# A hybrid decoder layer on one core: attention outputs copied by VectorE, a norm's scaling put last in its step, keys written a step later

## The chip, the core and the metric

The kernel runs on one core of a Trainium2 chip. The core has five engines that run at the same time, each through its own list of instructions in order: TensorE (PE, with its weight loads shown as PEld) multiplies matrices into PSUM banks; VectorE (DVE) and ScalarE (ACT) work on whole tiles of 128 partitions and can read PSUM; GpSimd (POOL) does element-wise work in SBUF; SyncE (SP) starts the DMA transfers. Engines wait for each other through semaphores. The metric is the device time of one execution in microseconds (us). Three runs of the kernel before gave 1030.6, 1030.78 and 1031.11; their median, 1030.78 us, is the time to compare with.

## The reference

One layer of a decoder on a sequence of 512 positions and a width of 1024, all in float32:

```python
u = rmsnorm(x, ln1_g)
q, k, v, pool_in, z, xbc, dt_raw, gate_pre = split(u @ w_in)
y_a = dilated_attention_mixer(q, k, v, rel_bias) @ w_a   # three groups of 6 heads, dilation 1, 4, 16
y_b = pool_mixer(pool_in, pool_w, pool_scale) @ w_b      # causal means over 2, 4, 8, 16 positions
y_c = ssd_mixer(z, xbc, dt_raw, ...) @ w_c               # state space scan in chunks of 128
gates = sigmoid(gate_pre + b_gate)
x = x + (gates[0] * y_a + gates[1] * y_b + gates[2] * y_c) @ w_o
x = x + conv_ffn(rmsnorm(x, ln2_g), ...)
return rmsnorm(x, final_g)
```

In the attention, each group's output `o` and the log-sum of its scores are computed by themselves, and the three outputs are summed with softmax weights over the groups. In the state space branch the result `y` is multiplied by `silu(z)`, normed over each of two halves of 512 channels (`y * rsqrt(mean(y*y) + eps) * norm_w`), and then multiplied by `w_c`.

## The kernel before

Every large product is done in three matmuls: each operand is split into a high half (a cast to a shorter float format, `wh`, `uh`, `ah`, `yth`) and a low half (the difference, `wl`, `ul`, `al`, `ytl`), and high x high, high x low and low x high are summed in PSUM (`mm3`, whose matmuls have line 237). Weights come as *jobs*: a DMA fetches a job's weights (`fetch`, L184), ScalarE casts the high half (`cast`, L196), VectorE subtracts to get the low half (`lows`, L216), and the job's body issues the matmuls. While one job's matmuls are issued, the next job's low half, the cast of the one after and the fetch of the one after that are issued ahead of them (`prepare`).

Smaller work is cut into generators. A job's body calls `step()` after each chunk of matmuls. A step takes one new generator from the list `waiting` into the list `running`, and moves each running generator on by one stretch, in the order of that list. Within the step there are phases: what stands before any other yield runs first, then what follows `yield ROWS`, then `yield WHOLE`, and last `yield REST`. A bare `yield` ends the generator's part of this step. `after(n, it)` lets n steps go by before `it` begins. Casts that were put off (`second`) are issued at the start of a step. Four engines run exactly in the order in which these Python lines issue instructions, so moving a line changes what each engine does first.

Tiles of 128 x 512 come from one pool of 54 slots, PSUM banks from two tags of four (`mm` for the chunks, `sm` for the small work). A new tile takes a slot that has come free and waits for its last reader.

Three places matter here:

- **Keys of the second attention group** (`qk_sevens(1)`). Queries and keys of dilation 4 are computed with seven half-size products in place of eight. The jobs run in the order A11, 4, A12, 1, 2, 3, A22. Job 2's evacuation is `p6`: VectorE adds the product to `r1` (L702), then `emit("k", 0, ...)` writes the first half of the keys, three additions of 128 x 256 in all (L695). Job 3's evacuation `p7` does the same for the second half (L707, L695), and A22 writes the second half of the queries. Gate jobs and the scores of `attend(1)` follow.
- **Outputs of the attention** (`attend(g)`). A pair of heads gives its scores (L743), which get their bias (L758), maximum (L762) and exponential (L765), are transposed (L772, copied out at L773) and multiplied by the values into a bank `po` (L784). L790 copies that bank to `o`, for groups 1 and 2 with the positions put back in their order. The third group (g = 2) runs between gate jobs and the items of the state space scan (`ssd_item`): transposes `pxs` (L1025), products `py` (L1070) and `pyo` (L1077), and on VectorE L1040, L1047, L1079, L1080, L1083.
- **Norm of the state space branch** (`y_norm(gi)`, once for each half). ScalarE casts the sum of squares, VectorE makes its low half (L1127), two matmuls with ones sum it over the partitions, ScalarE does Ln, Exp and Square (L1135 to L1137), VectorE refines (L1140, L1141). Two steps later the loop at L1144 scales two of four tiles of `y` (L1146), ScalarE casts them (L1148), and the next step subtracts for the low halves (L1153) before it scales the other two. Around the same time `combine` weights the attention outputs on GpSimd (L835), `split_o(c)` adds the three groups (L841, VectorE), casts `ah` (L843, ScalarE) and subtracts `al` (L846, VectorE), for the product with `w_a`. The product with `w_c` comes after that.

Of the kernel before, what the change touches and what calls it, by code (L numbers as in the profile page):

```python
# [83 lines left out]
def trunk(ctx: ExitStack, tc, out, x, rel_bias, ln1_g, w_in, b_gate, w_a, pool_w, pool_scale, w_b,  # L84
# [492 lines left out]
    def blocked(ap, g):  # L577
        return ap.rearrange("p (r j) -> p r j", r=4) if g == 0 else perm(ap, g)
# [71 lines left out]
    def qk_sevens(g):  # L650


        W = []
        quarter = lambda two, h: w_in[:, (C_Q, C_K)[h] + 384 * g:(C_Q, C_K)[h] + 384 * g + 384].rearrange(
            "(k two p) c -> two p k c", two=2, p=P)[two]
        chunks = ((0, 1), (2,))
        r1, r2, r3, r5 = {}, {}, {}, {}

        def load():
            for two in range(2):  # L660
                W.append(ypool.tile([P, 4, S], F32, name="w3", tag="xs")[:, :, :384])
                sp.dma_start(W[two], quarter(two, 1))

        def job(j, raw, form, use):
            def body(ws):
                wh, wl = ws
                parts = side_u(j)
                for i, ms in enumerate(chunks):
                    ps = MM("pq")
                    for n, m in enumerate(ms):  # L670
                        o = slice(m * P, (m + 1) * P)
                        mm3(ps[:, 256 * n:256 * n + 256], lambda k: wh[:, k, o], lambda k: wl[:, k, o],
                            lambda k: parts[k][0], lambda k: parts[k][1], range(4))
                    use(i, ps[:, :256 * len(ms)])
                step()
            new = Job([raw] if raw is not None else [], 4, 384, body)
            new.form = form
            if raw is None:
                new.load = lambda: None
            return new  # L680

        def keep(r):
            def use(i, ps):
                r[i] = T("rq")[:, :ps.shape[-1]]
                act.copy(r[i], ps)
            return use

        def emit(which, hi, i, a, b):

            for n, m in enumerate(chunks[i]):  # L690
                if (which, g, m) not in QK:
                    QK[which, g, m] = T(f"{which}{g}")
                view = (grouped if which == "q" else plain)(QK[which, g, m], g)
                piece = lambda t: perm(t[:, 256 * n:256 * n + 256], g)
                dve.tensor_tensor(view[:, :, 64 * hi:64 * hi + 64], piece(a), piece(b), OP.add)  # L695

        def p5(i, ps):
            keep(r5)(i, ps)
            dve.tensor_tensor(r2[i], r2[i], ps, OP.add)

        def p6(i, ps):
            dve.tensor_tensor(r1[i], r1[i], ps, OP.add)  # L702
            emit("k", 0, i, r1[i], r2[i])

        def p7(i, ps):
            r3[i] = T("rq")[:, :ps.shape[-1]]
            dve.tensor_tensor(r3[i], r1[i], ps, OP.add)  # L707
            emit("k", 1, i, r3[i], r5[i])

        one = job("A11", quarter(0, 0), None, keep(r1))  # L710
        two = job("A12", quarter(1, 0), None, lambda i, ps: emit("q", 0, i, r1[i], ps))
        three = job(4, None, lambda: W[1], keep(r2))
        one.then = lambda: diff(one.raw, W[0], one.raw)
        three.then = lambda: diff(W[0], W[1], W[0])
        two.then = lambda: diff(W[1], W[1], one.raw)
        return load, [one, three, two, job(1, None, lambda: one.raw, p5), job(2, None, lambda: W[1], p6),
                      job(3, None, lambda: W[0], p7), job("A22", None, lambda: diff(two.raw, two.raw, W[1]),
                                                          lambda i, ps: emit("q", 1, i, r3[i], ps))]

    def attend(g):  # L720
        nm, ls = both[:, :, :HEADS], both[:, :, 32:]
        if g == 0:
            banks = [[(1, 0, 2), (2, 1, 2)], [(3, 2, 2), (0, 0, 1)]]
        else:
            banks = [[(n, n, 1) for n in range(4)]]
        outs, probs, scores = {}, {}, {}

        def item(h, nb, bank):
            c, hh = h // 2, h % 2
            b = bias_of(g, h)  # L730
            off, spans = 0, []
            for n, kb, w in bank:
                spans.append((n, kb, w, off))
                off += w * P
            if hh == 0:

                q, k = QK["q", g, c], QK["k", g, c]
                yield ROWS
                pss = [SM("ps"), SM("ps")]
                for n, kb, w, o in spans:  # L740
                    for i in range(2):
                        r = slice(DH * i, DH * i + DH)
                        pe.matmul(pss[i][:, o:o + w * P], q[r, n * P:(n + 1) * P],  # L743
                                  k[r, kb * P:(kb + w) * P], start=True, stop=True)
                scores[c, nb] = pss
            yield REST
            ps = scores[c, nb][hh]
            total = off
            sb = T("sb")
            if g == 0 and total == 384:  # L750
                dve.tensor_tensor(sb[:, :256], ps[:, :256], b, OP.add)
                dve.tensor_tensor(sb[:, 256:384], ps[:, 256:384], b[:, P:], OP.add)
                for n, kb, w, off in spans:
                    dve.tensor_reduce(nm[:, n, h:h + 1], sb[:, off:off + w * P],
                                      AX.X, OP.max, negate=True)
            else:
                n = len(bank)
                dve.scalar_tensor_tensor(sb.rearrange("p (n c) -> p n c", n=n),  # L758
                                         ps.rearrange("p (n c) -> p n c", n=n), 0.125 if g == 1 else 1.0,
                                         b.unsqueeze(1).to_broadcast([P, n, S // n]), OP.mult, OP.add)  # L760
                n0 = bank[0][0]
                dve.tensor_reduce(nm[:, n0:n0 + n, h], sb.rearrange("p (n c) -> p n c", n=n),  # L762
                                  AX.X, OP.max, negate=True)
            for n, kb, w, off in spans:
                act.activation(sb[:, off:off + w * P], sb[:, off:off + w * P], AF.Exp,  # L765
                               bias=nm[:, n, h:h + 1], accum_out=ls[:, n, h:h + 1])
            yield
            yield
            yield WHOLE
            pt = SM("pt")  # L770
            for o in range(0, total, P):
                pe.transpose(pt[:, o:o + P], sb[:, o:o + P], eye)  # L772
            (act.copy if h % 2 else dve.tensor_copy)(sb[:, :total], pt[:, :total])  # L773
            probs[h, nb] = sb
            if h % 2 == 0:
                return
            yield
            if c not in outs:
                outs[c] = SM("po")
            po = outs[c]  # L780
            for n, kb, w, off in spans:
                for i in range(w):
                    for hh in range(2):
                        pe.matmul(po[DH * hh:DH * hh + DH, n * P:(n + 1) * P],  # L784
                                  V[g, kb + i][:, (2 * c + hh) * DH:(2 * c + hh + 1) * DH],
                                  probs[2 * c + hh, nb][:, off + i * P:off + (i + 1) * P],
                                  start=i == 0, stop=i == w - 1)
            if nb == len(banks) - 1:
                o = T(f"o{g}")
                act.copy(blocked(o, g), grouped(po, g))  # L790
                OT[g, c] = o

        def stats():
            yield WHOLE
            ps = SM("pst")
            for n in range(4):
                pe.transpose(ps[:32 + HEADS, n * P:(n + 1) * P], both[:, n, :], eye)
            for at, store, nme in ((0, NM, "nmT"), (32, LS, "lsT")):
                t = store[g] = T(nme)
                dve.tensor_copy(blocked(t[:HEADS], g), grouped(ps[at:at + HEADS], g))  # L800

        fill([item(2 * c + hh, nb, bank) for c in range(3) for nb, bank in enumerate(banks)
              for hh in range(2)] + [after(2, stats())])

# [316 lines left out]
    def y_norm(gi):  # L1121
# [20 lines left out]
        yield  # L1142
        yield
        for j in range(4):  # L1144
            y, m = Y[gi][:, j, :], 4 * gi + j
            dve.scalar_tensor_tensor(y, y, cst["dgc"][:, 8 + m:9 + m], r, OP.mult, OP.mult)  # L1146
            yh, yl = T("yth", F32R), T("ytl", F32R)
# [566 lines left out]
```

## Time and profile before

| | |
|---|---|
| median of three runs | 1030.78 us |
| the profiled execution's own time | 1031.29 us |
| its span, first to last instruction | 1029.5 us |
| TensorE busy | 1018.4 us (99%) |
| VectorE busy | 709.0 us (69%) |
| ScalarE busy | 494.1 us (48%) |
| GpSimd busy | 129.2 us (13%) |
| mean granted TensorE clock | 0.998 |

In the rows of the timeline the first two numbers are the start from the beginning of the span and the time that the row covers, both in us. Then come engine, line, operation, what is written and read, shapes, and how many instructions the row merges; in brackets is the time for which the engine stood idle before it and what it waited for. Rows of merged instructions run from the start of the first to the end of the last. Matmuls overlap in the pipeline, so that a single one of 512 columns shows 0.39 us while the next starts 0.23 us after it. Rows of groups have a count, the busy time and mean, or for one line the least, the median and the greatest duration in ns.

### The profile page before, as it was taken

The numbers are of one execution on the slowest core, as the hardware profiler recorded it, in microseconds if no ns is written. First come the engines' busy times: TensorE is split into PE (matmuls) and PEld (weight loads), VectorE is DVE, ScalarE is ACT, GpSimd is POOL, SyncE is SP. The second block draws the span as 40 slices with busy tenths as digits, with TensorE's granted clock in tenths as the row PEclk, the third lists the DMA queues.
The fourth block names the chain that finished last, engine by engine and source line by source line (L and its number), as shares of the span: only waits on it lengthen the run. The fifth ranks groups of instructions, "written<-read, shape, count | busy, mean of one in ns | idle before, by whom it ended". The sixth has DMA issues, their size and how long they took to land.

```text
span 1029.5 us, 13279 instructions
## 1 busy us (share of the span) xinstructions
PE 1018.4 (99%) x5282; PEld 859.5 (83%) x5282; DVE 709.0 (69%) x940; ACT 494.1 (48%) x790; POOL 129.2 (13%) x108
## 2 busy tenths in 40 slices
PE   9999999999999999999999999999999999999997
PEld 8998877899888888878887888898888888888885
DVE  6553566788756659676788756767778668685756
ACT  6432545454674364567576333545444434433434
POOL 1770000000000001000043501101111100111002
PEclk9999999999999999999999999999999999999999
DMA  8444312124422354542253625543232233421322
GB/s 258 148 127 140 104 61 75 31 87 139 123 82 82 87 150 111 144 132 61 77 160 120 199 82 206 176 143 114 82 123 82 84 118 109 140 82 41 123 82 82
DMA packets 113356, 117.62 MB, mean 114 GB/s; under 512 B 5235, under 2 KB 97206, under 8 KB 113295
## 3 DMA queue, kind: packets, MB, share of 16 engines
q1 hardware_dynamic: 112703, 115.92, 36.7%
q8 instruction: 41, 0.67, 0.3%
q10 hardware_dynamic: 592, 0.86, 0.2%
q14 instruction: 20, 0.16, 0.1%
HBM read 112.97 MB, written 2.22 MB: 112 GB/s over the span
## 4 chain that ended last, share of the span: by engine, by line
PE 90%; DVE 5%; ACT 3%; DMA 1%; issue 1%; ACTq 0%; DVEq 0%
PE pa L237 29%; PE pu L237 22%; PE pb L237 12%; PE pd L237 7%; PE pqk L237 6%; PE pa L1565 2%; PE pq L237 2%; PE pu L1369 1%; PE ps L743 1%; PE pt L772 1%; PE ppw L237 1%; PE po L784 1%; DMA al<-ad 1%; DVE xs L1146 1%; DVE wl L216 1%
## 5 line engine op out<-in xcount | busy, mean ns | idle before, releaser
L216 DVE TENSOR_TENSOR wl<-raw,wh 128x2048 fp32r<-128x2048 f32 (+3 forms) x95 | 220.3, 2320 | 52.9 <-ACT wh L196 44.1
L196 ACT CAST wh<-raw 128x1024 fp32r<-128x1024 f32 (+3 forms) x188 | 187.7, 1018 | 47.6 <-DVE raw L341 18.0
L1264 DVE SCALAR_TENSOR_TENSOR hc<-pu,fcol,hc 128x510 f32<-128x510 f32 x88 | 65.8, 748 | 55.6 <-ACT hc L1261 54.0
L237 PE MATMUL pa<-uh,wh 128*128 128x512 f32 x384 | 97.5, 396 | 0.0
L237 PE MATMUL pa<-ul,wh 128*128 128x512 f32 x384 | 94.9, 389 | 0.0
L237 PE MATMUL pa<-uh,wl 128*128 128x512 f32 x384 | 94.8, 389 | 0.0
L237 PEld LDWEIGHTS pa<-ul,wh 128*128 128x128 f32 x384 | 72.1, 188 | 15.1
L237 PEld LDWEIGHTS pa<-uh,wl 128*128 128x128 f32 x384 | 72.1, 188 | 15.0
L237 PE MATMUL pu<-uh,wh 128*128 128x512 f32 (+1 forms) x352 | 83.6, 379 | 0.0
L237 PE MATMUL pu<-ul,wh 128*128 128x512 f32 (+1 forms) x352 | 83.5, 379 | 0.0
L237 PE MATMUL pu<-uh,wl 128*128 128x512 f32 (+1 forms) x352 | 83.5, 379 | 0.0
L237 PEld LDWEIGHTS pa<-uh,wh 128*128 128x128 f32 x384 | 70.3, 188 | 14.0
L237 PEld LDWEIGHTS pu<-ul,wh 128*128 128x128 f32 x352 | 64.2, 188 | 12.5
L237 PEld LDWEIGHTS pu<-uh,wl 128*128 128x128 f32 x352 | 64.2, 188 | 12.5
L237 PEld LDWEIGHTS pu<-uh,wh 128*128 128x128 f32 x352 | 64.1, 188 | 12.4
L1261 ACT ACTIVATE hc<-pu,fcol,fcol 128x512 f32<-128x512 f32 x40 | 31.2, 780 | 79.6 <-PE pu L237 79.6
L1269 POOL TENSOR_TENSOR hc<-hc 128x512 f32<-128x512 f32 x22 | 30.9, 1403 | 289.1 <-DVE hc L1264 226.1
L1053 POOL TENSOR_TENSOR st<-st,dts 128x512 f32<-128x512 f32 x4 | 6.8, 1707 | 381.2 <-ACT st L1061 320.7
L765 ACT ACTIVATE sb<-sb,nmls 128x128 f32<-128x128 f32 (+1 forms) x72 | 30.1, 419 | 31.1 <-DVE nmls L762 18.3
L1162 ACT ACTIVATE sg<-pa,col 128x512 f32<-128x512 f32 x24 | 16.5, 688 | 38.1 <-PE pa L237 34.0
L1266 ACT ACTIVATE hc<-hc 128x512 f32<-128x512 f32 x22 | 13.9, 632 | 40.1 <-DVE hc L1264 40.1
L907 DVE SCALAR_TENSOR_TENSOR xs<-pa,col,xs 128x509 f32<-128x509 f32 (+2 forms) x24 | 18.0, 749 | 18.7 <-ACT xs L903 18.2
(380 smaller groups left out, 1874.3 us busy)
## 6 DMA issues: line engine op xcount, KB each, us to landing
raw<-in_w_in_dram SPq DMA_DIRECT2D x25, 1024.0 KB, 5.8
raw<-in_ffn_w_up_dram SPq DMA_DIRECT2D x22, 1024.0 KB, 5.2
raw<-in_w_o_dram SPq DMA_DIRECT2D x8, 1024.0 KB, 6.3
raw<-in_ffn_w_down_dram SPq DMA_DIRECT2D x8, 1024.0 KB
raw<-in_w_in_dram SPq DMA_DIRECT2D x14, 512.0 KB, 4.0
raw<-in_w_in_dram SPq DMA_DIRECT2D x6, 768.0 KB
raw<-in_w_b_dram SPq DMA_DIRECT2D x4, 1024.0 KB, 5.1
al<-ad SPq DMA_DIRECT2D x16, 256.0 KB, 8.6
```

Source lines behind the costliest of these rows:

```text
L196: act.copy(job.high[:, :, o], job.raw[:, :, o])
L216: (eng or dve).tensor_tensor(l[:, :, o], job.raw[:, :, o], h[:, :, o].bitcast(F32), OP.subtract)
L237: pe.matmul(ps, l, r, start=first and n == 0, stop=last and n == total - 1, skip_group_check=onto)
L743: pe.matmul(pss[i][:, o:o + w * P], q[r, n * P:(n + 1) * P], k[r, kb * P:(kb + w) * P], start=True, stop=True)
L765: act.activation(sb[:, off:off + w * P], sb[:, off:off + w * P], AF.Exp, bias=nm[:, n, h:h + 1], accum_out=ls[:, n, h:h + 1])
L907: dve.scalar_tensor_tensor(t[:, sh:], ps[:, :S - sh], col[:, o_cw + 12 * k + m:o_cw + 12 * k + m + 1], t[:, sh:], OP.mult, OP.add)
L1162: act.activation(s, ps, AF.Sigmoid, bias=col[:, o:o + 1])
L1261: act.activation(t, ps, AF.Identity, bias=ff["c1"][:, ff["b"] + m:ff["b"] + m + 1], scale=fw(2, m))
L1264: dve.scalar_tensor_tensor(t[:, sh:], ps[:, :S - sh], fw(k, m), t[:, sh:], OP.mult, OP.add)
L1266: act.activation(t, t, AF.Silu)
L1269: pool.tensor_tensor(a, a, t, OP.mult)
L1565: pe.matmul(first[2 * n + j][:, lo:hi], a[:, k, j * P:(j + 1) * P], b[:, k, lo:hi], start=a is wh and b is uh and k == 0, stop=a is wl and ...
```

## The change

Three edits. The first half of the keys is no longer written in `p6`, but by a small generator that starts in the step after the one that ends job 2's body. The three copies of `o` of the third attention group go to VectorE in place of ScalarE. In `y_norm`, a `yield REST` stands ahead of the first and the third scaling, so that each pair of scalings with its casts is issued in the last phase of its step rather than at the generator's place in the first phase.

```diff
+        def later(i):
+            emit("k", 0, i, r1[i], r2[i])
+            return
+            yield
+
         def p6(i, ps):
             dve.tensor_tensor(r1[i], r1[i], ps, OP.add)
-            emit("k", 0, i, r1[i], r2[i])
+            running.append(after(1, later(i)))
...
             if nb == len(banks) - 1:
                 o = T(f"o{g}")
-                act.copy(blocked(o, g), grouped(po, g))
+                (dve.tensor_copy if g == 2 else act.copy)(blocked(o, g), grouped(po, g))
                 OT[g, c] = o
...
         for j in range(4):
+            if j % 2 == 0:
+                yield REST
             y, m = Y[gi][:, j, :], 4 * gi + j
             dve.scalar_tensor_tensor(y, y, cst["dgc"][:, 8 + m:9 + m], r, OP.mult, OP.mult)
             yh, yl = T("yth", F32R), T("ytl", F32R)
```

## The prediction

> **What bounds the kernel now.** The page comes first: one engine is busy nearly throughout.
>
> ```profile
> span 1029.5 us, 13279 instructions
> ...
> PE 1018.4 (99%) x5282; PEld 859.5 (83%) x5282; DVE 709.0 (69%) x940; ACT 494.1 (48%) x790; POOL 129.2 (13%) x108
> ```
>
> TensorE is idle for 1029.5 - 1018.4 = 11.1 us of the span. No edit here takes a matmul away, so time can only come out of places where TensorE stands still. The view of TensorE's waits lists these by releaser (columns: total us, times, longest us):
>
> ```profile
> PE uT L1582 <- DVE diag L1594: 1.3, 2, 0.9
> ...
> PE pxs L1025 <- ACT o L790: 0.9, 1, 0.9
> PE pa L237 <- DVE al L846: 0.6, 1, 0.6
> PE pq L237 <- DVE wl L216: 0.3, 1, 0.3
> ```
>
> The first row is the start of the kernel, which the change leaves alone. The other three are single stalls, one each: transposes waiting for ScalarE's copy of an attention output, the attention projection waiting for a low half `al`, and the last key/query product waiting for a low half of weights. Each edit touches the order of work in front of one of them. So the question is how much of each stall goes and whether something new takes its place. Since the end of a matmul in this trace is modelled, I measure stalls from start to start, which comes out larger than the idle time in that view.
>
> **Keys of the first half, a step later (p6, `later`).** Timeline at the stall:
>
> ```profile
> 258.22 3.47 ACT L196 CAST wh<-raw 128x768 fp32r<-128x768 f32 x4 [3.55 <-DVE raw L341]
> 258.76 1.19 DVE L695 TENSOR_TENSOR k<-rq 128x256 f32<-128x256 f32 x2
> 260.31 0.62 DVE L695 TENSOR_TENSOR k<-rq 128x256 f32<-128x256 f32 x1
> 260.85 1.75 DVE L216 TENSOR_TENSOR wl<-raw,wh 128x1536 fp32r<-128x1536 f32 x1
> 261.75 0.64 PE L237 MATMUL pq<-ul,wh 128*128 128x256 f32 x4
> 262.66 0.74 PE L237 MATMUL pq<-uh,wl 128*128 128x256 f32 x4 [0.27 <-DVE wl L216]
> 263.24 0.64 PE L237 MATMUL pq<-uh,wh 128*128 128x256 f32 x4
> 265.31 2.28 DVE L216 TENSOR_TENSOR wl<-raw,wh 128x2048 fp32r<-128x2048 f32 x1
> 269.77 1.97 PE L237 MATMUL pa<-uh,wl 128*128 128x512 f32 x8
> ```
>
> Groups of four such matmuls follow each other by 0.48 us where nothing waits: a group of four takes 0.64, of which the last matmul's tail overlaps the next group. From 261.75 two groups would bring the third to 262.71; it starts at 263.24. The stall with its restart costs 0.53 us. It ends when L216, the last job's split, ends at 262.60. In front of that split VectorE does three key writes, 1.19 + 0.62 = 1.81 us, and these are what moves. The split cannot go forward by all of it: it also needs ScalarE's cast. Of the four casts the first two are this job's, so by half of 3.47 us they are done near 259.95. The split then runs from about 259.95 to 261.70, before 262.23 when TensorE asks. The stall goes: gain 0.53.
>
> What comes later: the same three writes run at the end of the next step, between the other keys and the gate's split at 265.31. VectorE has gained nothing but a gap before the cast (260.85 - 259.95 = 0.9 earlier against 1.81 taken out), so that split ends 0.9 later, at 268.5 instead of 267.6. TensorE wants it at 269.77 - 0.53 = 269.24; 0.7 us of cover is left. The scores that read these keys come behind the gate's whole first chunk, whose last part starts at 269.77; the keys are written near 266.3 by then. No DMA is issued by the moved part, and no queue of SP or POOL is passed. Bounds of this term: 0.43 without the restart, 0.53 with it.
>
> **Outputs of the third group by VectorE (`attend(2)`, L790).** There are three such copies. The first is the one TensorE waits for; an undisturbed step is shown ahead of it.
>
> ```profile
> 442.00 1.16 PE L1077 MATMUL pyo<-xcv,st 128*128 128x128 f32 x8
> 442.99 0.60 PE L1025 MATMUL pxs<-eye,xs 128*128 128x128 f32 x4
> 443.35 0.94 PE L237 MATMUL pa<-uh,wh 128*128 128x512 f32 x3
> 457.06 1.04 PE L784 MATMUL po<-sb,vr 128*64 128x128 f32 x16
> 458.03 1.16 PE L1077 MATMUL pyo<-xcv,st 128*128 128x128 f32 x8
> 458.91 1.08 ACT L790 COPY o<-po 128x512 f32<-128x512 f32 x1
> 459.22 0.69 DVE L1079 TENSOR_TENSOR ea<-pyo,ea 128x512 f32<-128x512 f32 x1 [1.49 <-PE pyo L1077]
> 460.04 0.66 PE L1025 MATMUL pxs<-eye,xs 128*128 128x128 f32 x4 [0.86 <-ACT o L790]
> 460.45 0.71 PE L237 MATMUL pa<-uh,wh 128*128 128x512 f32 x2
> 464.55 0.68 DVE L1040 TENSOR_SCALAR al<-al,acs 128x128 f32<-128x128 f32 x3 [2.14 <-DMA al<-ad]
> ```
>
> From pyo to the next projection takes 443.35 - 442.00 = 1.35 us undisturbed and 460.45 - 458.03 = 2.42 here: 1.07 lost, because the transposes take over the bank of `po`, ScalarE, busy with other work, begins its copy only at 458.91. VectorE is idle just then (1.49). In the written order the copy stands ahead of L1047 and L1079, so VectorE goes to it when `po` ends at 457.06 + 1.04 = 458.10. How long does it take there? The same pattern (grouped in, blocked out) appears on VectorE for six rows, and plain copies out of PSUM on both engines:
>
> ```profile
> L800 DVE COPY lsT<-pst x3: 682/1049/1053, 194.6 to 504.9; 6x512 f32<-6x512 f32 x3
> L773 DVE COPY sb<-pt x12: 547/683/692, 132.6 to 492.9; 128x512 f32<-128x512 f32 x9, 128x384 f32<-128x384 f32 x3
> L773 ACT COPY sb<-pt x12: 451/577/590, 135.8 to 498.2; 128x512 f32<-128x512 f32 x9, 128x384 f32<-128x384 f32 x3
> ```
>
> I take 1.05 to 1.07, the nearest row: 458.13 to 459.20, transposes at 459.25 with the latency seen at 459.99 to 460.04. They start 0.79 earlier; 0.23 and the restart stay. Bounds: 683 ns would end before the transposes could start at all (gain 1.07). If VectorE is slower than ScalarE in the strided case as in the plain one, 683/577 x 1.08 = 1.28 us, the gain is 0.58. The Trainium skill speaks for this dearer price (VectorE: DVE Perf Modes, Specifications: ScalarE is placed closer to PSUM, VectorE closer to SBUF). The plain rows agree with it by 18%; with it the whole sum below would be 0.21 smaller, but the 1.049 row is strided and on VectorE, so I stay with that.
>
> What queues behind the waiting copy: L1047 (two multiplies), then L1079 and its followers, some 1.4 us later than now. L1040, which comes next, waits 2.14 for a DMA until 464.55 anyway, which covers it. ScalarE is rid of 1.08 three times, worth nothing alone: TensorE waits for none of the other two copies. They cost VectorE about 1.07 each, in steps for which the view of TensorE's waits has no row; should that cover be gone, each costs at most its 1.07.
>
> **Scaling last in its step (`y_norm`, `yield REST`).** The order of VectorE before the third stall:
>
> ```profile
> 544.29 3.48 DVE L1146 SCALAR_TENSOR_TENSOR xs<-xs,dgc,yr 128x512 f32<-128x512 f32 x2
> 547.70 3.48 DVE L841 TENSOR_TENSOR o<-o,o 128x512 f32<-128x512 f32 x2
> 553.30 1.28 DVE L1153 TENSOR_TENSOR ytl<-xs,yth 128x512 fp32r<-128x512 f32 x2
> 556.48 0.69 DVE L1140 SCALAR_TENSOR_TENSOR yt<-pss,yt 128x512 f32<-128x512 f32 x1 [1.89 <-ACT yt L1137]
> 564.25 1.41 DVE L1146 SCALAR_TENSOR_TENSOR xs<-xs,dgc,yr 128x512 f32<-128x512 f32 x2
> 564.46 0.84 PE L237 MATMUL pa<-ah,wh 128*128 128x512 f32 x3
> 565.14 0.61 PE L237 MATMUL pa<-al,wh 128*128 128x512 f32 x2
> 565.58 0.68 DVE L846 TENSOR_TENSOR al<-o,ah 128x512 fp32r<-128x512 f32 x1
> 566.32 0.50 PE L237 MATMUL pa<-al,wh 128*128 128x512 f32 x1 [0.56 <-DVE al L846]
> 566.65 0.63 PE L237 MATMUL pa<-ah,wl 128*128 128x512 f32 x2
> 581.66 1.98 PE L237 MATMUL pa<-yth,wh 128*128 128x512 f32 x8
> ```
>
> Three such matmuls take 565.14 - 564.46 = 0.68 start to start, so `ah,wl` was due at 565.82 and started at 566.65: 0.83 lost to the third `al` (565.58 to 566.26, wanted at 565.60). In that step two scalings, 1.41 us, run right ahead of it; last in the step they run behind it, and `al` is ready at 564.85. That alone suffices. The step at 544 helps too: `o` goes before the scalings, so ScalarE's `ah` and the Ln, Exp and Square behind it start some 3.4 us earlier and the 1.89 of waiting at L1140 goes. Against that, the two later low halves (L1153) now wait for casts that ScalarE does after these functions, by my count some 0.4 us at 553.3; net some 1.5 us earlier. So even with TensorE ahead by the other two gains (0.53 + 0.79 = 1.32, wanting `al` at 564.28) it is there at about 563.4. The scaled `y` is first read at 581.66, over ten microseconds after the last scaling, which is the cover for the delay. The moved scalings issue no DMA; their cast on ScalarE moves with them. Gain 0.83, bounds 0.56 to 0.83.
>
> **Sum.** 0.53 + 0.79 + 0.83 = 2.15 us. The profiled execution itself took 1031.29 (its span and 1.79 around it), so it would take 1029.14. The median of the runs is 0.51 below the profiled one: 1030.78 - 2.15 = 1028.63. Low ends 0.43 + 0.58 + 0.56 = 1.57 give 1029.2; high ends 0.53 + 1.07 + 0.83 = 2.43 give 1028.35.
>
> **Rivals.** (1) One stall stays because what it waits for is not earlier: most likely `al` (ScalarE's `ah` comes later than I counted) or the transposes (the copy starts late behind another VectorE operation). Against it: VectorE's idle 1.49 and the 1.41 that suffices by itself. One term of about 0.8 falls away: 1029.4. (2) The change doesn't do what it says: TensorE is early after each place, and asks early for the next split, cast or DMA, which hands all of it back; 1030.8. Against it: after the last stall no wait of TensorE is listed at all. (3) The other side: VectorE's tightest place, the gate's split with 0.7 us of cover. Tiles come from one pool of 54 slots in the order in which these come free, and the moved writes change who gets which; a write that lands on a slot whose last reader is late holds VectorE in front of that split. The longest wait that VectorE shows in front of a split is 7.7:
>
> ```profile
> DVE wl L216 <- ACT wh L196: 46.0, 32, 7.7
> ```
>
> Such a wait there would cost 7.7 - 0.7 = 7.0, and the sum 7.0 - 2.15 = 4.9 slower, 1035.6; it decides from 0.7 + 2.15 + 2.06 = 4.9 us of lateness. Nothing in the trace shows one.
>
> **How the numbers follow.** A measurement here tells about 0.2%, 2.06 us, from no change: the bound is 1028.72. All three stalls go: 0.72 (own range 1028.3 to 1029.2, as just worked out), and since its centre lies 0.09 below the bound with the dearer copy above it, 0.50 of that falls under the bound and 0.22 above. One stall stays: 0.15. All handed back: 0.05. Slower: 0.08. So faster 0.50, same 0.22 + 0.15 + 0.05 = 0.42, slower 0.08. The range 1028.1 to 1030.0 takes in the first two cases with 0.2 us for the scatter of the runs, and leaves out the last two and a little below.
>
> **What would show it.** In the changed kernel's waits of TensorE the rows for L237 <- L216 and L237 <- L846 are gone, and pxs waits 0.1 to 0.3 us for a VectorE copy of some 1.07 us that starts at the end of `po`. The three key writes stand after the second half's, and L216 for the last key/query job starts when its cast ends. I am wrong if TensorE's idle time falls by less than 1 us, if the copy takes over 1.3 us, or if a wait not in the list above appears behind 265 us.

## The result: 1.1 us, half of what was predicted

The changed kernel takes 1029.68 us (median of 22 runs, 1029.19 to 1030.25) beside 1030.80 us for the kernel before (22 runs, 1029.87 to 1031.76). The ratio is 0.9988, with an interval of 0.9983 to 0.9994: 1.12 us or 0.11% faster, which is less than the 0.2% that was set as the bound of no change. The interval is 0.6 to 1.8 us of gain; no gain at all lies outside it, and so do the 2.15 us of the prediction. The prediction was 1028.6, with a range of 1028.1 to 1030.0.

The two profiled executions say something else. The kernel before took 1031.29 and the changed one 1029.19, which is 2.10 apart and almost exactly the predicted 2.15. Why one pair of traces and the medians differ by a factor of two is what most of the experiments are about.

The page of the changed kernel (span, busy time, and its chain that ended last) shows the gain where it was looked for:

```profile
span 1027.4 us, 13279 instructions
...
PE 1017.5 (99%) x5282; PEld 859.4 (84%) x5282; DVE 710.5 (69%) x943; ACT 490.8 (48%) x787; POOL 129.1 (13%) x108
...
PE 98%; DMA 1%; DVE 0%; ACT 0%; ACTq 0%; issue 0%
```

The same line of the chain, on the page of the kernel before:

```profile
PE 90%; DVE 5%; ACT 3%; DMA 1%; issue 1%; ACTq 0%; DVEq 0%
```

TensorE's idle time fell from 11.1 us to 1027.4 - 1017.5 = 9.9. That is only 1.2 less, because part of each stall counts as busy: the busy time fell too, by 0.9, with the same 5282 matmuls. VectorE and ScalarE have left the chain. The view of TensorE's waits in the changed kernel has lost all three rows at issue and gained none; what is left is the start of the kernel:

```profile
PE uT L1589 <- DVE diag L1601: 1.7, 2, 1.1
PE pa L1530 <- DVE ones L1521: 1.1, 1, 1.1
```

Now the three places in the changed kernel's timeline, in the order of the prediction. Line numbers are 5 higher from L700 on and 7 higher from L1150 on. First the keys:

```profile
259.88 1.76 DVE L216 TENSOR_TENSOR wl<-raw,wh 128x1536 fp32r<-128x1536 f32 x1 [0.76 <-ACT wh L196]
261.81 0.64 PE L237 MATMUL pq<-ul,wh 128*128 128x256 f32 x4
...
262.77 0.64 PE L237 MATMUL pq<-uh,wh 128*128 128x256 f32 x4
263.81 2.24 DVE L695 TENSOR_TENSOR k<-rq 128x256 f32<-128x256 f32 x4
265.97 2.29 DVE L216 TENSOR_TENSOR wl<-raw,wh 128x2048 fp32r<-128x2048 f32 x1
269.31 1.07 PE L237 MATMUL pa<-uh,wl 128*128 128x512 f32 x4
```

Groups of four now follow by 0.48 us throughout (261.81, 262.29, 262.77). The group that started at 261.75 before starts at 261.81, and the one two later at 262.77 instead of 263.24: 0.47 + 0.06 = 0.53 gained. Then the copy:

```profile
456.59 1.04 PE L789 MATMUL po<-sb,vr 128*64 128x128 f32 x16
457.56 1.16 PE L1082 MATMUL pyo<-xcv,st 128*128 128x128 f32 x8
457.68 1.08 DVE L795 COPY o<-po 128x512 f32<-128x512 f32 x1 [4.37 <-PE po L789]
458.60 2.12 DVE L1052 TENSOR_TENSOR al<-al,cbt 128x512 f32<-128x512 f32 x2
458.81 0.66 PE L1030 MATMUL pxs<-eye,xs 128*128 128x128 f32 x4
459.23 2.08 PE L237 MATMUL pa<-uh,wh 128*128 128x512 f32 x8
```

VectorE starts the copy 0.05 us after `po` ends, and the transposes start 1.25 after `pyo` (458.81 - 457.56) where they started 2.01 after it (460.04 - 458.03). The next projection starts at 459.23 instead of 460.45: 1.22 earlier in all, 0.75 of it new here. And the norm:

```profile
541.87 3.48 DVE L846 TENSOR_TENSOR o<-o,o 128x512 f32<-128x512 f32 x2
545.27 3.48 DVE L1153 SCALAR_TENSOR_TENSOR xs<-xs,dgc,yr 128x512 f32<-128x512 f32 x2
553.18 0.68 DVE L1145 SCALAR_TENSOR_TENSOR yt<-pss,yt 128x512 f32<-128x512 f32 x1
560.95 0.68 DVE L851 TENSOR_TENSOR al<-o,ah 128x512 fp32r<-128x512 f32 x1
561.55 1.41 DVE L1153 SCALAR_TENSOR_TENSOR xs<-xs,dgc,yr 128x512 f32<-128x512 f32 x2
564.61 0.84 PE L237 MATMUL pa<-ah,wl 128*128 128x512 f32 x3
```

The sums `o` and their followers go ahead of the scalings, both at 541.87 and at 560.95. L1145 starts with no wait in front of it. The third `al` ends at 561.63. The group `ah,wl`, which stands right behind the matmul that reads it, starts at 564.61 instead of 566.65, 2.04 earlier, 0.82 of it new. So in these two executions the three terms are 0.53, 0.75 and 0.82, against 0.53, 0.79 and 0.83 predicted.

### The profile page after: what moved, and what is told of

The parts are those of the page before. It is cut to its first block, busy times and chain, and to the rows that moved or that the text cites. A ratio compares the mean times of both kernels' runs of the same rounds, so it can differ in the third digit from the quotient of the medians.

```text
span 1027.4 us, 13279 instructions
## 1 busy us (share of the span) xinstructions
PE 1017.5 (99%) x5282; PEld 859.4 (84%) x5282; DVE 710.5 (69%) x943; ACT 490.8 (48%) x787; POOL 129.1 (13%) x108
## 4 chain that ended last, share of the span: by engine, by line
PE 98%; DMA 1%; DVE 0%; ACT 0%; ACTq 0%; issue 0%
PE pa L237 36%; PE pu L237 22%; PE pb L237 12%; PE pd L237 7%; PE pqk L237 6%; PE pq L237 3%; PE pa L1572 2%; PE ps L748 1%; PE pu L1376 1%; PE pt L777 1%; PE po L789 1%; PE ppw L237 1%; PE py L1075 1%; DMA xin<-in_x_dram 1%; PE pyo L1082 1%; PE pst L1063 0%
## 5 line engine op out<-in xcount | busy, mean ns | idle before, releaser
L237 PE MATMUL pa<-uh,wh 128*128 128x512 f32 x384 | 97.5, 396 | 0.0
L237 PE MATMUL pa<-ul,wh 128*128 128x512 f32 x384 | 94.9, 389 | 0.0
L237 PE MATMUL pa<-uh,wl 128*128 128x512 f32 x384 | 94.8, 389 | 0.0
L237 PEld LDWEIGHTS pa<-ul,wh 128*128 128x128 f32 x384 | 72.1, 188 | 15.1
L237 PEld LDWEIGHTS pa<-uh,wl 128*128 128x128 f32 x384 | 72.1, 188 | 15.0
L237 PE MATMUL pu<-uh,wh 128*128 128x512 f32 (+1 forms) x352 | 83.6, 379 | 0.0
L237 PE MATMUL pu<-ul,wh 128*128 128x512 f32 (+1 forms) x352 | 83.5, 379 | 0.0
L237 PE MATMUL pu<-uh,wl 128*128 128x512 f32 (+1 forms) x352 | 83.5, 379 | 0.0
L237 PEld LDWEIGHTS pa<-uh,wh 128*128 128x128 f32 x384 | 70.3, 188 | 14.0
L237 PEld LDWEIGHTS pu<-ul,wh 128*128 128x128 f32 x352 | 64.2, 188 | 12.5
L237 PEld LDWEIGHTS pu<-uh,wl 128*128 128x128 f32 x352 | 64.2, 188 | 12.4
L237 PEld LDWEIGHTS pu<-uh,wh 128*128 128x128 f32 x352 | 64.1, 188 | 12.4
```

What stands on the lines that cost most here:

```text
L237: pe.matmul(ps, l, r, start=first and n == 0, stop=last and n == total - 1, skip_group_check=onto)
```

## The experiments

Two theories stood against each other in the end. By that of the prediction, each edit takes its own stall away, and the medians differ from the traces by scatter. By the other (D in the expectations, formed after the first four runs), the copies' stall is not a property of the kernel before but of its one traced execution. "Time" below is the median of 8 to 11 runs; the kernel before beside them gave medians of 1031.00, 1031.01 and 1031.06 (31 to 33 runs each). The lag from `pyo` to the transposes `pxs` is from start to start.

| kernel | time, us | ratio to before | pyo to pxs, us | split of keys late | third `al` late |
|---|---|---|---|---|---|
| before (traced once) | | 1 | 2.01 | yes | yes |
| the change, second trace | 1029.51 | 0.9985 (0.9977 to 0.9994) | 1.25 | no | no |
| keys alone | 1030.24 | 0.9993 (0.9984 to 1.0002) | 1.25 | no | yes |
| copies alone | 1030.34 | 0.9991 (0.9982 to 1.0000) | 1.25 | yes | no |
| norm alone | 1030.21 | 0.9992 (0.9983 to 1.0001) | 1.25 | yes | no |
| keys and norm | 1029.64 | 0.9989 (0.9980 to 0.9997) | 1.25 | no | no |
| 2 loads ahead, ScalarE copies | 1030.42 | 0.9994 (0.9985 to 1.0003) | 1.25 | yes | yes |
| 2 loads ahead, VectorE copies | 1030.02 | 0.9991 (0.9982 to 1.0000) | 1.25 | yes | no |
| 6 loads ahead, ScalarE copies | 1031.99 | 1.0007 (0.9998 to 1.0017) | 1.95 | yes | yes |
| 6 loads ahead, VectorE copies | 1030.21 | 0.9992 (0.9983 to 1.0002) | 1.27 | yes | no |
| norm, second half only | 1030.15 | 0.9989 (0.9979 to 1.0000) | 1.27 | yes | no |
| three products on GpSimd | 1030.02 | 0.9991 (0.9981 to 1.0002) | 1.25 | yes | no |
| the change, `uh` cast first | 1029.33 | 0.9985 (0.9976 to 0.9994) | 1.26 | no | no |

**Each edit alone, and the whole again.** The keys alone:

```diff
-            emit("k", 0, i, r1[i], r2[i])
+            running.append(after(1, later(i)))
```

> Only the keys' edit. Both theories expect the product that waited for the split (0.53 us late before) on time, and the gate's split behind it ending near 268.5 us, before TensorE asks. Theory S (the stalls are the same in every execution): the other two stalls stand in this trace as before, 1.07 us at the transposes and 0.83 us at the third al, and the time falls by 0.5 us. Rival V (the stalls vary from execution to execution, and the traced execution of before had long ones): one of those two differs from its value before by over 0.2 us, and the time falls by 0.3 us or less.

The copies alone:

```diff
-                act.copy(blocked(o, g), grouped(po, g))
+                (dve.tensor_copy if g == 2 else act.copy)(blocked(o, g), grouped(po, g))
```

> Only the copies' edit. Both theories: the first VectorE copy takes 1.05 to 1.1 us, starts when po ends, and the transposes are 0.2 to 0.35 us late instead of 1.07. S: the split stall (0.53) and the third al (0.83) stand as before; the time falls by 0.8 us. V: one of them differs by over 0.2 us; the time falls by 0.4 us or less.

The norm alone:

```diff
         for j in range(4):
+            if j % 2 == 0:
+                yield REST
```

> Only the norm's edit. Both theories: the third al is there before TensorE asks for it. S: the split stall (0.53) and the transposes (1.07) stand as before; the time falls by 0.8 us. V: one of them differs by over 0.2 us; the time falls by 0.4 us or less.

And the whole change once more:

> The whole change once more, traced anew. S: the time falls by 2.1 us, as between the two traced executions, and this trace lies within 0.2 us of the first one at every point of TensorE's order. V: the time falls by 1.1 us, as between the medians, and the trace shows where an execution gets longer: a stall of 0.2 us or more that the first trace does not have, at the kernel's start or in the middle.

The edits alone gave -0.76, -0.66 and -0.79 us against 1031.00; they add up to -2.21, and the whole gave -1.49. Each of these numbers has some 0.9 us of uncertainty, so the times alone don't settle it. By the marks set beforehand neither S nor V came out whole. In each of the three traces one stall is gone that its edit doesn't touch, as V said, but the times fell by 0.66 to 0.79 us, nearer to S's 0.5 to 0.8 than to V's 0.4 or less. The traces tell more. With the keys edit alone, ScalarE still makes the copy, and the transposes are not late:

```profile
448.58 1.72 DVE L1045 TENSOR_SCALAR al<-al,acs 128x128 f32<-128x128 f32 x8 [1.40 <-DMA al<-ad]
453.69 0.40 ACT L770 ACTIVATE sb<-sb,nmls 128x128 f32<-128x128 f32 x1
457.23 1.04 ACT L196 CAST wh<-raw 128x1024 fp32r<-128x1024 f32 x1
458.11 1.16 PE L1082 MATMUL pyo<-xcv,st 128*128 128x128 f32 x8
458.23 1.08 ACT L795 COPY o<-po 128x512 f32<-128x512 f32 x1
459.36 0.66 PE L1030 MATMUL pxs<-eye,xs 128*128 128x128 f32 x4
```

The same stretch in the one trace of the kernel before:

```profile
450.53 1.68 DVE L1040 TENSOR_SCALAR al<-al,acs 128x128 f32<-128x128 f32 x8 [3.42 <-DMA al<-ad]
...
453.64 0.69 DVE L762 TENSOR_REDUCE nmls<-sb 128x4 f32<-128x512 f32 x1
...
454.43 0.40 ACT L765 ACTIVATE sb<-sb,nmls 128x128 f32<-128x128 f32 x1 [0.72 <-DVE nmls L762]
...
457.98 1.03 ACT L196 CAST wh<-raw 128x1024 fp32r<-128x1024 f32 x1
```

This is the chain that the prediction missed. There the DMA of `al` for the scan item landed late: it was issued at 441.37, beside 441.15 in the trace above, and VectorE waited for it 3.42 us until 450.53 (448.58 above). Behind it in VectorE's order stand the bias and the maximum of the next scores (L758, L762). ScalarE waited 0.72 for that maximum, and its exponentials, sigmoid, weight cast and the copy of `o` all came 0.7 later: the copy at 458.91 instead of 458.23. ScalarE is busy up to the copy in the trace above too, but there its cast ends at 458.27, 0.1 after `po` (457.13 and 1.04 in that trace), and the copy is in time. There is no cover, so what the late DMA added in this execution counted in full.

The third stall goes in two ways. With the copies alone it is gone too, without any edit of the norm. GpSimd's products begin at 535.97 there instead of 535.07, on the arrival of the weights `wb`, and so after the first pair of scalings has begun; that pair takes 2.44 us instead of 3.48. The other two kernels with VectorE's copies and no norm edit, further down, agree (536.35 and 536.12, no third stall); the three others with ScalarE's copies and no norm edit begin at 534.36 to 535.27 and have the stall. The traces show the link in VectorE's order. Its third copy of `o` (503.06) stands ahead of the work that ends in the weights: the reciprocal (L822) starts at 518.41 instead of 517.65, GpSimd's products behind it (L826) at 521.89 instead of 521.13, and the first load of `wb` is issued at 529.62 instead of 528.70, though TensorE was 0.2 earlier there. VectorE in the kernel with the copies alone:

```profile
535.45 2.44 DVE L1146 SCALAR_TENSOR_TENSOR xs<-xs,dgc,yr 128x512 f32<-128x512 f32 x2
...
562.88 1.41 DVE L1146 SCALAR_TENSOR_TENSOR xs<-xs,dgc,yr 128x512 f32<-128x512 f32 x2
564.20 0.68 DVE L846 TENSOR_TENSOR al<-o,ah 128x512 fp32r<-128x512 f32 x1
```

The scalings still stand ahead of the third `al`, but it ends at 564.88 instead of 566.26. So copies and norm each remove the same 0.83, and their single gains can't be added. The prediction's theory falls in this form: the gain to expect from the whole is 0.53 + 0.83 = 1.36, which lies within the intervals of both medians, with 0.76 more in an execution whose `al` lands as late as in the trace of before.

**The change without the copies.** D says that it runs like the whole change.

> The change without its copies: ScalarE still copies the third group's outputs. Theory D: ScalarE's copy is late only when the DMA of al lands late; where VectorE's L1040 starts by 449.8 us, the transposes start 1.25 us after pyo, as with VectorE's copy. Then the copies are worth nothing in most executions and this kernel takes the time of the whole change, 1.1 to 1.5 us below before. Rival Q: ScalarE's copy is late by its place in ScalarE's queue, in every execution; the transposes start about 2.0 us after pyo, and the time is 0.8 us above the whole change.

It takes 1029.64, beside 1029.68 and 1029.51 for the whole change. ScalarE's copy there starts when `po` ends:

```profile
457.98 1.16 PE L1082 MATMUL pyo<-xcv,st 128*128 128x128 f32 x8
458.10 1.08 ACT L795 COPY o<-po 128x512 f32<-128x512 f32 x1
459.23 0.66 PE L1030 MATMUL pxs<-eye,xs 128*128 128x128 f32 x4
```

The difference in time can't be told from nothing (the intervals reach some 0.9 us to each side); the lag in the trace is the same 1.25.

**Landing made late by loads ahead of it.** If D holds, a kernel whose `al` is sure to come late should pay with ScalarE's copy and not with VectorE's. Additional loads go ahead of the DMA of `al` in the same queue, into tiles that nothing reads. The keys and norm edits are absent from all four kernels.

```diff
+        if (c, gi) == (2, 1):
+            for i in range(2):
+                sp.dma_start(T("late"), x[i * P:(i + 1) * P, :S])
         for q in range(2):
             al = T("al")
```

> The kernel before with two loads of 256 KB (into a tile that nobody reads) in front of the al transfers of the one scan item whose transposes run at 443 us, so that these land some 2 to 4 us later. D: L1040 starts at 450.5 to 453 us, and the transposes at 458 start later than 1.25 us after pyo by L1040's start minus 449.8, so 2 to 4.5 us after pyo. Q: no such relation; about 2.0 us whatever L1040 does.

> The same two loads with VectorE's copies and nothing else of the change. D: VectorE takes the copy when po ends as long as L1040 starts before about 452.1 us (its split L216, which ends 6.0 us after L1040's start, is then done by the end of po); the transposes start 1.25 us after pyo. If L1040 starts later than 452.1, they are late by the difference. Time below late_scalar by the difference of the two stalls. Q: the same 1.25.

Two loads were too few: VectorE began L1040 at 448.65 and 449.18, within what other traces show without them, and both lags are 1.25. This pair decides nothing. With six loads (`range(6)`, the rows taken in turn):

> The kernel before with six loads of 256 KB in front of the same al transfers (two delayed them too little). From the traces so far, ScalarE's copy starts 6.7 us after VectorE ends L1040, or when po ends if that is later. D: L1040 ends 2.5 to 4 us later than the 449.7 to 451.0 us of the traces with a 1.25 us gap, near 453.5; the copy then starts near 460.2 and the transposes 3.3 us after pyo (2 to 5), some 2 us more than the undelayed case. Q: no relation; 1.25 or 2.0.

> The same six loads with VectorE's copies and nothing else of the change. D: the split ahead of the copy ends 4.3 us after L1040, near 457.8, so that VectorE is free when po ends: the transposes start 1.25 to 1.6 us after pyo, and the time lies 1.5 to 3 us below later_scalar, of which up to 0.8 is the third al. Q: no difference at the transposes between the two kernels.

L1040 now began at 451.54 and 452.46. ScalarE's copy with six loads:

```profile
458.43 1.16 PE L1080 MATMUL pyo<-xcv,st 128*128 128x128 f32 x8
...
459.63 0.69 DVE L1082 TENSOR_TENSOR ea<-pyo,ea 128x512 f32<-128x512 f32 x1 [0.69 <-PE pyo L1080]
460.06 1.10 ACT L790 COPY o<-po 128x512 f32<-128x512 f32 x1
...
460.38 0.65 PE L1028 MATMUL pxs<-eye,xs 128*128 128x128 f32 x4 [0.79 <-DVE ea L1082]
```

And VectorE's copy with six loads:

```profile
458.76 1.16 PE L1080 MATMUL pyo<-xcv,st 128*128 128x128 f32 x8
458.88 1.10 DVE L790 COPY o<-po 128x512 f32<-128x512 f32 x1 [0.26 <-PE po L784]
...
460.03 0.66 PE L1028 MATMUL pxs<-eye,xs 128*128 128x128 f32 x4
```

The late landing delays ScalarE's copy by 1.5 us against its undisturbed place 0.12 after `pyo` starts (460.06, where D had worked out 460.2), and doesn't touch VectorE's. That much of D holds. What the late copy would have cost TensorE this pair does not show. The transposes here took over another bank, that of `pyo`, and didn't wait for the copy at all: they waited for L1082, which reads that bank and began as soon as `pyo` had ended. So the 1.95 comes from the bank and not from the landing; D had expected 3.3, and Q's 2.0 fits the number as well. Why the bank is another one the trace doesn't tell. That a late copy of ScalarE holds up the transposes is therefore seen in one trace only, that of the kernel before. The times lie 1.78 us apart; 0.68 of it is the difference of the lags and 0.83 the third `al`, which is late in the first kernel only. The rest of 0.27 is within the scatter.

**Does the 1.41 us alone suffice?** Only the second half's scalings are moved:

```diff
+            if j % 2 == 0 and gi == 1:
+                yield REST
```

> The norm's edit for the second half of the channels only (the two scalings that stood right ahead of the third al). If these 1.41 us alone suffice, the third al ends near 564.9 us and TensorE does not wait; the split stall of 0.53 stands. If the order in the step at 544 us is what counts, the third al stays late by over 0.5 us.

Yes. VectorE reaches the third `al` in the same order as before up to 564.24, and the pair of scalings is behind it; TensorE lists no wait for it:

```profile
564.24 0.69 DVE L846 TENSOR_TENSOR al<-o,ah 128x512 fp32r<-128x512 f32 x1
564.84 1.41 DVE L1148 SCALAR_TENSOR_TENSOR xs<-xs,dgc,yr 128x512 f32<-128x512 f32 x2
```

**What made VectorE late there in the first place.** Two scalings cost 3.48 us at 544.29 and 1.41 at 564.25 in the kernel before. GpSimd's nine products run beside the first pair and not beside the second. Here GpSimd multiplies only the first group, and the other two are summed without their weights:

```diff
+                if g == 0:
-                pool.tensor_tensor(OT[g, c], OT[g, c], wb, OP.mult)
+                    pool.tensor_tensor(OT[g, c], OT[g, c], wb, OP.mult)
```

> The kernel before with GpSimd's products for the first attention group only, three instead of nine (the outputs of the other two groups are summed without their softmax weights). If GpSimd at work is what makes VectorE's operations take 1.74 us in place of 0.7, the nine operations from the first scaling to the last addition of o take 9 to 11 us instead of 15.3, and the third al is on time by several us. If they are slow for another reason, they take 15 us again and the third al is late as before.

VectorE at the same work, mostly between GpSimd's products (537.29 to 538.73 and from 542.52 on):

```profile
540.41 1.40 DVE L1147 SCALAR_TENSOR_TENSOR xs<-xs,dgc,yr 128x512 f32<-128x512 f32 x2
541.74 1.41 DVE L842 TENSOR_TENSOR o<-o,o 128x512 f32<-128x512 f32 x2
```

The pairs that took 3.48 each take 1.40 and 1.41. The stretch from the first scaling to the end of the `o` sums (nine VectorE operations) takes 8.0 us (535.14 to 543.15) instead of 15.4 (535.78 to 551.18), and the third `al` ends at 559.23, five microseconds ahead of its use. So the stall needs both: without six of the nine products `al` is in time in the old order, and with all nine it is in time in the new one.

**Another wait.** In several traces, though not in the first one of the changed kernel, TensorE waits near 684 us. The timeline of the kernel with the keys edit alone:

```profile
681.87 2.00 ACT L196 CAST wh<-raw 128x1024 fp32r<-128x1024 f32 x2 [5.95 <-DMA raw<-in_ffn_w_up_dram]
683.77 1.07 ACT L456 CAST uh<-uT 128x512 fp32r<-128x512 f32 x2
684.39 0.88 PE L237 MATMUL pu<-uh,wh 128*128 128x256 f32 x5 [0.42 <-ACT uh L456]
```

ScalarE waits for a DMA of up-weights, then casts them for 2 us, and only then casts the `uh` that TensorE wants first. The landing differs from one execution to the next, and the wait with it (0.2 to 0.4 us in the four kernels whose waits of TensorE list it, 0.4 to 0.7 from start to start). So the weights' cast was put behind the `uh` casts, on top of the whole change:

```diff
+                        if later == "hold":
+                            held_cast.append(lambda: cast(weights[n + 2], 2))
+                        else:
+                            cast(weights[n + 2], 2, spread=not later)
...
+                else:
+                    held_cast.pop()()
```

> The whole change, and beside it one cast of weights for the up projection (two instructions of ScalarE) issued behind the casts of uh2's last blocks instead of ahead of them. Theory U: the 0.1 to 0.7 us by which the first full up product started late in four of the traces (near 684 us) come from ScalarE holding that cast for a weight transfer while uh waits behind it; here the product starts on time, within 0.1 us, and the time falls by 0.2 to 0.5 us against the whole change. Rival: the lateness of the transfer comes back at the next use of those weights, and the time stays.

```profile
680.21 1.08 ACT L456 CAST uh<-uT 128x512 fp32r<-128x512 f32 x2 [5.75 <-PE uT L453]
681.17 2.00 ACT L196 CAST wh<-raw 128x1024 fp32r<-128x1024 f32 x2
```

The order is as meant. Its median of 1029.33 is the lowest of all kernels here, 0.2 to 0.35 below the two medians of the change, which these runs can't tell from nothing. The first trace of the change has no wait there either, so that one trace without it doesn't show that the new order prevents it.

## Why the prediction was half right

**Keys: right in place and size.** The split began at 259.88 (259.95 said) and ended near 261.64 (261.70). The gain was 0.53. The gate's split ended at 268.26 instead of 268.5, 1.05 us ahead of its use, so the rival of 1035.6, in which VectorE is held up in front of it, didn't occur.

**Copies: the mechanism right, the size wrong.** This is the step that failed: "They start 0.79 earlier", taken from a single execution and carried to the median. That VectorE would start at the end of `po` came true, and it took 1.08 where 1.05 to 1.07 was said; the dearer price of 1.28 by the plain rows did not come. The Trainium skill (VectorE: DVE Perf Modes, Specifications) places ScalarE closer to PSUM; in this strided form the traces show no advantage of it, 1.08 on either engine. But of eight traces with ScalarE's copy, counting the one before, only two show transposes more than 1.27 behind `pyo`: that one, and the one with six loads ahead, whose lag came from another bank. In the six others the term is 0 to 0.02. The sum against the median should have been 0.53 + 0.83 = 1.36, or 1029.4. The sign was in the trace of the kernel before, though not in the rows that the prediction quotes: ScalarE's 0.7 of idle time waiting for L762, and the DMA wait of 3.42 that set L762, lie just ahead of the copy, and the copy's start was put down to "other work" without following it back. The 0.51 by which the median lay below the profiled execution was subtracted as a constant; what it is made of was not asked.

**Norm: right in place and size, wrong in what it depends on.** The gain was 0.82 in the traces, and the 1.41 alone suffices, as claimed. With the norm's edit alone the third `al` ended at 563.32, beside the 563.4 worked out; the wait of 1.89 at L1140 went, and 0.20 of the 0.4 of new waiting at the low halves appeared. In the whole change it came at 561.63, mostly because TensorE and the work tied to it are 1.2 ahead there. Unseen was that the copies edit removes the same stall through GpSimd's start, so that the terms are not independent. In the sum this did no harm, because the stall was counted once.

**The rest of the difference.** From trace to trace it was 2.10 and from median to median 1.12 and, in the second set of runs, 1.49. The trace of before lies 0.49 above its median of 1030.80, and the first trace of after 0.49 below its own. The late landing is not the whole account of the first, because executions also differ at the start. The second L442 of VectorE waits for a DMA of `x`; here in the kernel before and in the one with the norm alone, which are the same up to there:

```profile
7.34 0.69 DVE L442 SCALAR_TENSOR_TENSOR junk<-xin 128x512 f32<-128x512 f32 x1 [0.47 <-DMA xin<-in_x_dram]
8.26 0.69 DVE L442 SCALAR_TENSOR_TENSOR junk<-xin 128x512 f32<-128x512 f32 x1 [1.26 <-DMA xin<-in_x_dram]
```

TensorE's first product of L237 starts at 36.73 in the trace of before, at 36.79 in the first of after, and anywhere from 36.70 to 37.51 in the fourteen traces. The two traces compared first both had an early start and no loss near 684 us, so that their 2.10 is made of the three stalls alone. The trace of the keys alone lies 1.11 above its median without any late copy: against the trace of before it lost 0.61 at the start and 0.69 near 684. The second trace of the changed kernel (1029.66) lost 0.47 against the first, 0.25 of it near 245 us and 0.2 near 684. None of these places was in the prediction. The start and 245 us come ahead of anything that the edits move. None of the three edits is needed for the loss near 684, since each edit is absent from at least two of the kernels that show it. Whether TensorE's being early makes it likelier these traces don't tell: of the two in which TensorE was not ahead by then (the trace of before itself, and the one with six loads and ScalarE's copies), one shows no loss and one 0.1; of the eleven in which it was (leaving out the one with `uh` cast first), five show 0.2 to 0.7.

By the prediction's own marks the second trace is a close case: TensorE's idle time there is 10.1 us, 1.0 less than before, where a fall of less than 1 was to show it wrong, and the view of its waits has no row for the 0.2 near 684.

**The rivals.** The first one's 1029.4 is the nearest number to what was measured, yet its case (a stall that stays) did not happen: all three rows are gone. That the median lies inside the range of 1028.1 to 1030.0 is therefore in part luck: its upper part was there for that case. No trace shows a new wait in every execution that hands the gain back. What stays open is how often `al` lands late in the kernel before; only one of its executions was traced.

## What to carry to other kernels

A stall of under 1 us in one traced execution is priced only after its chain is followed back to the end: where it starts at a DMA, its size belongs to that execution, and the median may have none of it. Where the profiled execution lies above the median, the difference alone doesn't say which stall to suspect: here it was 0.49 with the late copy and 1.11, in the kernel with the keys alone, without it. Gains at places that share a later engine are added only after each edit has been traced alone.

## What the runs showed of the hardware

VectorE and GpSimd take turns when both work on two tiles in SBUF. GpSimd in the kernel before, a single product in the scan and the nine of `combine`:

```profile
459.27 1.04 POOL L1053 TENSOR_TENSOR st<-st,dts 128x512 f32<-128x512 f32 x1 [29.52 <-PE pyo L1077]
```

```profile
535.07 15.57 POOL L835 TENSOR_TENSOR o<-o,wb 128x512 f32<-128x512 f32 x9 [7.24 <-DMA wb<-wd]
```

A product takes 1.04 us by itself and 15.57 / 9 = 1.73 in the row of nine; a VectorE operation of this size takes 0.69 by itself (0.70 in the kernel with three products) and 1.74 beside them. 0.69 + 1.04 = 1.73: each pair takes the time of both, one after the other. The Trainium skill (SBUF — State Buffer, Who interferes with whom) says that a VectorE instruction with two SBUF inputs contends with a GpSimd instruction that reads SBUF, and that the shared ports are an exclusive lock; the trace agrees, with these numbers. The copies edit pays for it once: VectorE's two multiplies at L1052 fall beside GpSimd's product and take 2.12 us instead of 1.29, where nothing waits for them.

The second finding is scatter. In kernels with no added loads VectorE ended L1040, which waits for the DMAs of the same `al`, between 448.92 (the change) and 452.21 us (before). In the kernel with the norm's second half alone it ended at 452.13, as late as in before, and yet the transposes came 1.27 after `pyo`: TensorE was 0.67 later there (`pyo` at 458.70 instead of 458.03), after a start slower by the same 0.67. So what counts is the landing against TensorE's own position. It cost TensorE 0.76 us in the trace of before and at most 0.02 in the others without added loads.
